# Twelve weight tiles of the convolution stage split on GpSimd, fewer float32 tiles, and a residual without alpha

## The chip, the cores and the metric

The kernel runs on one core of a Trainium2 chip. The metric is the device time of one execution in microseconds (us). The five engines of the core run their own instruction streams and wait for one another by semaphores: TensorE (PE in the profile; its weight loads are PEld), VectorE (DVE), ScalarE (ACT), GpSimd (POOL) and SyncE (SP), which here issues the DMAs.

## The reference, cut to what matters

Two blocks follow one another on x of 256 tokens by 1024 channels, all in float32. The change lies in the second block, in its first half:

```python
h = layer_norm(x) * (1.0 + sc1[:, None]) + sh1[:, None]
proj = h @ w_in                                   # 1024 x 4096
a_val, a_gate, u_pool, gate_a, gate_b = split(proj)   # 512, 512, 512, 1024, 1024 columns ...
ya = a_val * sigmoid(a_gate)
ya = causal_dwconv(ya, w_dw_a, b_dw_a)            # 31 taps, per channel
ya = silu(layer_norm(ya, ln_a_g, ln_a_b))
ya = ya @ w_pw_a
yb = einsum(causal_multiscale_pool(u_pool), w_pool) * pool_scale
merged = sigmoid(gate_a) * ya + sigmoid(gate_b) * yb
mix = merged @ w_out
x = layer_norm(ALPHA * x + g1[:, None] * mix, ln1_g, ln1_b)   # ALPHA = 2 ** 0.25
```

The layer norm adds LN_EPS = 1e-5 to the variance. A common factor on its input drops out of it, if the added number is scaled by the factor's square.

## The kernel before, in words

Activations lie transposed, channels on the 128 partitions and 256 tokens along the free dimension, in blocks of 128 channels. A weight tile is 128x1024 float32 (eight blocks of 128x128, 512 KB), fetched by one DMA from the SP queue into a buffer named `raw`. A product of a 128x128 block with 256 tokens is made in one of two ways:

- **split** (`mm`, lines 237 to 239): weights and activations are each held as a rounded part and a rest (`wh` and `wl` for weights), and three matmuls of the fast float32 form are added: wh by high, wh by low, wl by high. `load` makes the two weight parts from `raw`: ScalarE copies with rounding (line 178, `wh<-raw`), VectorE subtracts (line 179, `wl<-raw,wh`). There are five `wh`, five `wl` and six `raw` buffers.
- **float32** (`mm32`, line 243): one matmul in plain float32 (two records in the trace), with no work for the other engines. Such a tile is fetched straight into a `wh` or `wl` buffer.

The stage of the change runs on PE in this order. `ahead_mm` makes four tiles of w_in in float32 from input that is not yet normed. `k_outer` makes four split tiles. Then come 20 tiles of w_in by `in_tile`: four for the pool branch, all float32, and eight pairs (i = 0 to 7) for the gates; pairs 2, 5 and 6 are split and pairs 0, 1, 3, 4 and 7 are float32, so 14 tiles in all are float32. After pair 3 come 24 matmuls of the pool branch (`pool_out`), which need the pooled sums from VectorE. After pair 7 comes `half_outer("w_pw", ...)`, which needs the normed convolution (`yap`).

Beside it run the 31 taps of the convolution, in two halves of two channel blocks. In 53 of its 62 steps ScalarE multiplies two blocks by their tap (line 1087) and VectorE adds the pair to `acc` (line 1088, 128x512, both inputs in SBUF); in seven VectorE does both (line 1091), and two start the sum (line 1083). The steps are written into the program by a clock that counts planned PE time: `every(0.9, 62, conv)` puts one step every 0.9 us of it. The scheduler of the language then sets the order on each engine. After the last step come the sums of the layer norm on PE (line 1178), its statistics, and `yap` (lines 1186 to 188). For the residual, ScalarE makes `ax` = ALPHA times x (line 1120) in four instructions of 128x512 just ahead of the convolution, and VectorE later adds g1 times mix to it (`fin_mix`).

GpSimd sets a few margins to zero (line 1065, for the pool branch), issues five DMAs, and adds two tiles at the very end (line 1432).

Of the kernel before, what the change touches and what calls it, by code (L numbers as in the profile page):

```python
# [11 lines left out]
F32 = mybir.dt.float32  # L12
F32R = mybir.dt.float32r
I32 = mybir.dt.int32
AF = mybir.ActivationFunctionType
ALU = mybir.AluOpType
ADD, SUB, MUL = ALU.add, ALU.subtract, ALU.mult
AX = mybir.AxisListType

P = 128  # L20
S = 256
D = 1024
DB = D // P
RMS_EPS = 1e-6
LN_EPS = 1e-5
ALPHA = 2.0 ** 0.25
# [55 lines left out]
@with_exitstack  # L82
def tile_kernel(ctx, tc, order, xT, pT, pos, vec, cst, cv, rows, wada, wts, outT):
    nc = tc.nc
    V, A, T = nc.vector, nc.scalar, nc.tensor

    cp = ctx.enter_context(tc.tile_pool(name="cp", bufs=1))
    hp_ = ctx.enter_context(tc.tile_pool(name="half", bufs=14))
# [8 lines left out]
    def nm(s):  # L97
        uid[0] += 1
        return f"{s}_{uid[0]}"
# [4 lines left out]
    def bank2():  # L104
        return bank().rearrange("p (b t) -> p b t", b=2)

    class Blk:

        def __init__(self, nb, dt=F32):
            self.t = [hp_.tile([P, 4, S], dt, tag="half", name=nm("half")) for _ in range((nb + 3) // 4)]  # L110
# [26 lines left out]
    def t1(dt=F32, tag="t1", bufs=8):  # L137
        return tp.tile([P, S], dt, tag=tag, name=nm("t1"), bufs=bufs)
# [3 lines left out]


    class Seq:
        def __init__(self, entries, width=P, parts=True, ready=()):
            self.e, self.w, self.i, self.parts, self.ready = entries, width, 0, parts, list(ready)

        def next(self):
            per = D // self.w
            s = self.i % per  # L150
            if s == 0:
                self.h, self.l = load(self.e[self.i:self.i + per], self.w, self.parts, self.ready.pop(0) if self.ready else None)
            self.i += 1
            sl = slice(s * self.w, (s + 1) * self.w)
            return self.h[:, sl], self.l[:, sl]

    def fetch(entries, width, parts=True, step=D, pinned=False):
        g = len(order)
        order.append((width, list(entries)))
        n = len(entries) * width  # L160
        tag, bufs = (("raw", 6), ("wh", 5), ("wl", 5))[0 if parts else [0, 1][g % len([0, 1])]]
        raw = wp.tile([P, D], F32, tag=tag, name=nm("raw"), bufs=bufs)
        for o in range(0, n, step):
            e = min(n, o + step)
            d = nc.sync.dma_start(out=raw[:, o:e], in_=wts[g, :, o:e])
            if pinned:
                tc.keep_in_program_order(d)
        return raw[:, :n]

    def load(entries, width, parts=True, raw=None):  # L170
        if raw is None:
            raw = fetch(entries, width, parts)
        if not parts:
            return raw, raw
        n = raw.shape[1]
        hi = wp.tile([P, D], F32R, tag="wh", name=nm("wh"), bufs=5)[:, :n]
        lo = wp.tile([P, D], F32R, tag="wl", name=nm("wl"), bufs=5)[:, :n]
        A.copy(hi, raw)  # L178
        V.tensor_sub(lo, raw, hi.bitcast(F32))  # L179
        return hi, lo  # L180

    def nouter(name, ms, kbs, c0=0):
        return [(name, kb * P, c0 + m * P) for m in ms for kb in kbs]
# [19 lines left out]
    def after(us, fn):  # L203
        queue.append((clk[0] + us, fn))
        queue.sort(key=lambda e: e[0])
# [40 lines left out]
    def rhs(pair, kb):  # L246
        return pair[0][kb], pair[1][kb]


    xt = Blk(DB)  # L250
# [27 lines left out]
    V.memset(eps_r, RMS_EPS)  # L278
    eps_l = cp.tile([P, 1], F32, name="eps_l")
    V.memset(eps_l, LN_EPS)  # L280
    A.copy(cp.tile([P, 1], F32, name="first"), eps_l)

    def col(name, i, n=1):
# [81 lines left out]
    def newton(r0, ve, out, eps=None):  # L365
        t = t1()
        V.tensor_mul(t, r0, r0)
        u = t1()
        if eps is None:
            V.tensor_mul(u, ve, t)  # L370
        else:
            V.scalar_tensor_tensor(u, ve, eps, t, ADD, MUL)
        V.scalar_tensor_tensor(out, u, 3.0, r0, SUB, MUL)
        return out
# [6 lines left out]
        A.activation(r0, ps, AF.Abs_reciprocal_sqrt, bias=eps_r, scale=1.0 / n)  # L381
        return newton(r0, ve, t1(tag="nr", bufs=3) if out is None else out)

    def ln_stats(ps, n):

        mu = t1(tag="mu", bufs=2)
        A.activation(mu, ps[0], AF.Copy, scale=1.0 / n)
        msq = t1()
        A.activation(msq, ps[0], AF.Square, scale=1.0 / n)
        var = t1()  # L390
        V.scalar_tensor_tensor(var, ps[1], 1.0 / n, msq, MUL, SUB)
        r0 = t1()
        A.activation(r0, var, AF.Abs_reciprocal_sqrt, bias=eps_l)
        return mu, newton(r0, var, t1(tag="nr", bufs=3), eps=LN_EPS)

    def bc2(t, n=2):
        return t.unsqueeze(1).to_broadcast([P, n, S])
# [2 lines left out]
    mod = cp.tile([P, 48], F32, name="mod")  # L400
# [22 lines left out]
    def every(us, n, step):  # L423

        def run():
            step()
            if n > 1:
                every(us, n - 1, step)
        after(us, run)
# [59 lines left out]
    r0 = {}  # L489
# [251 lines left out]
    xt = post(xt, ys, sums, 0, prep)  # L741
# [56 lines left out]
    seq = Seq([e for kb in range(8) for e in (("mla_kr", kb * P, 0), ("mla_in", kb * P, 768), ("mla_in", kb * P, 896))])  # L798
# [9 lines left out]
    seq = Seq(nouter("mla_in", range(6), range(8)))  # L808
    for i in range(3):
        ps = bank2()  # L810
# [144 lines left out]
    xt = post(xt, ys, sums, 1, prep)  # L955
# [8 lines left out]
    def mod_scales(w):  # L964
        sl = slice(8 * w, 8 * w + 8)
        V.tensor_scalar(s1[:, sl], mod[:, 8 + 24 * w:16 + 24 * w], 1.0, None, ADD)
        V.tensor_scalar(ms[:, sl], s1[:, sl], -0.5, None, MUL)
# [57 lines left out]
    def k_outer(name, tiles, pair):  # L1025
        seq = Seq([(name, kb * P, m * P) for kb in range(8) for m in tiles])
        banks = [bank2() for _ in range(len(tiles) // 2)]
        for kb in range(8):
            for i in range(len(tiles)):
                mm(banks[i // 2][:, i % 2, :], seq.next(), rhs(pair, kb), kb == 0 and i % 2 == 0, kb == 7 and i % 2 == 1)  # L1030
        return banks
# [5 lines left out]
    st = {}  # L1037
# [6 lines left out]
    mu, nrl = st["in"]  # L1044
# [64 lines left out]
    def glu_ahead(i):  # L1109
        gt, gw = ahead_out(pab[2 * i + 1])  # L1110
        A.activation(gt, gt, AF.Sigmoid, bias=gw)
        vt, vw = ahead_out(pab[2 * i])
        V.scalar_tensor_tensor(apad[:, i, 30:], vt, vw, gt, ADD, MUL)
# [1 line left out]
    glu_ahead(0)  # L1115
    modulate(xt, 0, mu, nrl, range(2, 4), hp, hraw)
    glu_ahead(1)
    ax = Blk(DB)
    for i in range(4):
        A.activation(ax.pair(i), xt.pair(i), AF.Copy, scale=ALPHA)  # L1120
    every(0.9, 62, conv)
    pab = k_outer("w_in2", [2, 6, 3, 7], hp)
    for i in (2, 3):
        glu(pab[i - 2], i)

    def in_tile(ps, m, parts):
        seq = Seq(nouter("w_in2", [m], range(8)), parts=parts)  # L1130
        for kb in range(8):
            if parts:
                mm(ps, seq.next(), rhs(hp, kb), kb == 0, kb == 7)
            else:
                mm32(ps, seq.next()[0], hraw[kb], kb == 0, kb == 7)

    for i in range(2):
        ps = bank2()
        for b in range(2):
            in_tile(ps[:, b, :], 8 + 2 * i + b, False)  # L1140
        for b in range(2):
            A.copy(up[2 * i + b][:, 16:], ps[:, b, :])
    pq = Blk(4)
# [61 lines left out]
    for i in range(8):  # L1205
        j = (i + 4) % 8
        ps = bank2()
        for b in range(2):
            in_tile(ps[:, b, :], 12 + 2 * j + b, bool(100 >> i & 1))
        A.activation(sab.pair(j), ps, AF.Sigmoid)  # L1210
        if i == 3:
            pool_out()
# [8 lines left out]

    half_outer("w_pw", yap, fin_pw, 4)

    z = Blk(DB)
    mod_scales(1)
    gs = cp.tile([P, 8], F32, name="gs")
    V.tensor_mul(gs, s1[:, 8:16], col("ln1_g_2", 0, 8))
# [6 lines left out]
    sumz = Sums(True, 1)  # L1234

    def fin_mix(ps, k0, n):
        for b in range(n):
            k = k0 + b
            V.scalar_tensor_tensor(z[k], ps[:, b, :], mod[:, 16 + k:17 + k], ax[k], MUL, ADD)
            A.activation(zs[k][:, :S], z[k], AF.Copy, scale=gs[:, k:k + 1])  # L1240
        if n == 2:
            sumz.feed(z.span(k0, 2))
            if k0 == 4:
                after(4.16, sumz.flush)
        else:
            if k0 == 7:
                drain()
                after(2.03, lambda: (sumz.end(z.span(7, 1), True), ln_1()))
            else:
                after(1.0, lambda: sumz.end(z.span(6, 1), False))  # L1250
# [28 lines left out]
        st["x1"] = ln_stats(sumx.ps[::-1], D)  # L1279

    def ln_1():
        st["z"] = ln_stats(sumz.ps[::-1], D)

        def part(k, n):
            if n == 2:
                sumx.feed(x1.span(k, 2))
        ln_affine(z, st["z"], 0, "ln1_b_2", x1, [1, 3, 5, 7], True, part)
        after(10.0, ln_2)
# [65 lines left out]
    seq = Seq([e for i in range(NA + 2, FB) for e in nouter("w_up", [i, FB + i], range(8))])  # L1354
    for i in range(NA + 2, FB):
        ps = bank2()
# [12 lines left out]
    seq = Seq([("w_down", kb * P, 512 * n) for kb in kbs for n in range(2)], 512)  # L1369

    chunks = [[(0, 512), (512, 512)], [(0, 512), (512, 256), (768, 256)]]
    ps = {(tb, o): bank()[:, :w] for tb in range(2) for o, w in chunks[tb]}
# [27 lines left out]
    for tb in range(2):  # L1400
# [17 lines left out]
        r0 = small(1)  # L1418
# [88 lines left out]
```

## Time and profile before

| what | us |
|---|---|
| median of 3 runs | 845.04 (843.58 to 845.37) |
| the profiled execution | 842.56 |
| its span from first to last instruction | 840.8 |
| PE, PEld busy in the span | 823.7 (98%), 787.2 (94%) |
| DVE, ACT, POOL busy | 702.4 (84%), 552.7 (66%), 9.9 (1%) |

Busy time of an engine is the time in which one of its instructions ran; matmuls overlap, so a busy PE can still differ in pace. The float32 tiles of the stage can be seen in the timeline of PE as unbroken rows of line 243 between 527.9 and 599.7 us. The clock that was granted to TensorE is 1.00 of full speed there, its upper level of 2.4 GHz.

### The profile page before, as it was taken

How to read it: one execution, taken by the hardware profiler on the slowest of the kernel's cores; microseconds unless marked ns; L12 is line 12 of the kernel's file. 1: busy time of each engine (PE TensorE's matmuls, PEld its weight loads, DVE VectorE, ACT ScalarE, POOL GpSimd, SP SyncE). 2: the span in 40 equal slices, each digit the busy share in tenths (PEclk: the TensorE clock that was granted, in tenths of full speed). 3: DMA queues.
4: the chain of work that ended last, by engine and by line, in shares of the span. 5: the costliest groups of instructions: out<-in, count | busy, mean ns of one | idle time of the engine just before them, and what ended most of it. 6: DMA issues, size and time to landing. Idle time of an engine off the chain costs nothing.

```text
span 840.8 us, 15768 instructions
## 1 busy us (share of the span) xinstructions
PE 823.7 (98%) x6114; PEld 787.2 (94%) x6114; DVE 702.4 (84%) x1283; ACT 552.7 (66%) x966; POOL 9.9 (1%) x30
## 2 busy tenths in 40 slices
PE   8999999999999999998999999999999999999995
PEld 6989899999999999998999999899998999999885
DVE  6999798988889978688864767899677888889986
ACT  7655565555676787777754867998755576666551
POOL 0000000000000000000000000000000000000001
PEclk9999999999999999999999999999999999999999
DMA  9876567779556647364354355246363455567822
GB/s 333 330 253 221 206 225 273 253 267 323 174 176 249 250 149 255 135 242 150 109 181 176 118 209 176 76 174 196 132 240 113 148 188 191 179 220 252 274 79 76
DMA packets 46634, 167.48 MB, mean 199 GB/s; under 512 B 5216, under 2 KB 5472, under 8 KB 46560
## 3 DMA queue, kind: packets, MB, share of 16 engines
q1 hardware_dynamic: 45936, 164.38, 55.6%
q0 software_dynamic: 624, 2.10, 0.8%
q8 instruction: 48, 0.79, 0.4%
q14 instruction: 26, 0.21, 0.1%
HBM read 165.41 MB, written 1.05 MB: 198 GB/s over the span
## 4 chain that ended last, share of the span: by engine, by line
PE 51%; DVE 2%; ACT 1%; issue 1%; DVEq 0%
PE ps L238 13%; PE ps L237 13%; PE ps L239 13%; PE ps L243 10%; PE ps L341 1%; PE ps L363 0%; DVE wl L179 0%; PE ps L920 0%; PE ps L1170 0%; DVE t L1434 0%; DVE sm L1415 0%; DVE half L690 0%; DVE t L1411 0%; DVE t L1412 0%; PE ps L1407 0%
## 5 line engine op out<-in xcount | busy, mean ns | idle before, releaser
L237 PE MATMUL ps<-half,wh 128*128 128x256 f32 x1504 | 426.2, 284 | 0.0
L238 PE MATMUL ps<-half,wh 128*128 128x256 f32 x1504 | 424.0, 282 | 0.7 <-DVE half L188 0.6
L239 PE MATMUL ps<-half,wl 128*128 128x256 f32 x1504 | 422.2, 281 | 0.0
L178 ACT CAST wh<-raw 128x1024 fp32r<-128x1024 f32 x233 | 243.5, 1049 | 156.9 <-PE ps L238 99.7
L179 DVE TENSOR_TENSOR wl<-raw,wh 128x1024 fp32r<-128x1024 f32 x233 | 283.1, 1222 | 61.4 <-ACT wh L178 59.3
L238 PEld LDWEIGHTS ps<-half,wh 128*128 128x128 f32 x1504 | 283.6, 189 | 2.0 <-DVE half L188 1.1
L237 PEld LDWEIGHTS ps<-half,wh 128*128 128x128 f32 x1504 | 283.1, 188 | 1.1 <-ACT half L187 0.5
L239 PEld LDWEIGHTS ps<-half,wl 128*128 128x128 f32 x1504 | 284.0, 189 | 0.0
L243 PE MATMUL ps<-half,raw 128*128 128x256 f32 (+2 forms) x384 | 84.9, 380 | 0.0
L243 PEld LDWEIGHTS ps<-half,raw 128*128 128x128 f32 x384 | 72.6, 190 | 9.9
L237 PE MATMUL ps<-wh,half 128*128 128x512 f32 (+1 forms) x202 | 72.7, 361 | 1.0 <-ACT wh L178 1.0
L238 PE MATMUL ps<-wl,half 128*128 128x512 f32 (+1 forms) x202 | 71.1, 352 | 0.5 <-DVE wl L179 0.5
L239 PE MATMUL ps<-wh,half 128*128 128x512 f32 (+1 forms) x202 | 71.1, 352 | 0.0
L413 DVE CUSTOM_DVE_ANT_0 adach<-adach,siluc 128x1024 f32<-128x1024 f32 x48 | 58.6, 1222 | 13.8 <-DMA adach<-in_wada 13.8
L1087 ACT ACTIVATE t<-apad,vec 128x256 f32<-128x256 f32 x106 | 44.3, 500 | 0.5 <-DVE half L1088 0.5
L237 PEld LDWEIGHTS ps<-wh,half 128*128 128x128 f32 x202 | 38.0, 188 | 6.8 <-ACT wh L178 1.8
L238 PEld LDWEIGHTS ps<-wl,half 128*128 128x128 f32 x202 | 38.1, 189 | 6.0 <-DVE wl L179 1.0
L239 PEld LDWEIGHTS ps<-wh,half 128*128 128x128 f32 x202 | 38.0, 188 | 5.6
L1088 DVE TENSOR_TENSOR half<-half,t 128x512 f32<-128x512 f32 x53 | 36.6, 690 | 3.7 <-ACT t L1087 1.8
L187 ACT CAST half<-t 128x256 fp32r<-128x256 f32 (+1 forms) x47 | 20.6, 454 | 18.1 <-DVE t L1347 10.9
L188 DVE TENSOR_TENSOR half<-t,half 128x256 fp32r<-128x256 f32 (+1 forms) x47 | 21.8, 485 | 4.0 <-ACT half L187 3.0
L1342 ACT ACTIVATE t<-ps,vec 128x256 f32<-128x256 f32 x38 | 21.0, 557 | 2.0 <-PE ps L239 1.2
(290 smaller groups left out, 905.5 us busy)
## 6 DMA issues: line engine op xcount, KB each, us to landing
raw<-in_wts SPq DMA_DIRECT2D x257, 512.0 KB, 4.1
adach<-in_wada SPq DMA_DIRECT2D x48, 512.0 KB, 5.0
half<-in_xT SPq DMA_DIRECT2D x4, 256.0 KB, 6.0
half<-in_rows POOLq DMA_DIRECT2D x2, 512.0 KB, 4.5
out<-t SPq DMA_DIRECT2D x4, 256.0 KB, 2.0
cst<-in_cst SPq DMA_DIRECT2D x1, 928.0 KB, 10.6
raw<-in_wts SPq DMA_DIRECT2D x2, 256.0 KB, 4.2
siluc<-in_cv SPq DMA_DIRECT2D x1, 512.0 KB, 8.5
```

Of the source, the lines that this page charges most:

```text
L178: A.copy(hi, raw)
L179: V.tensor_sub(lo, raw, hi.bitcast(F32))
L187: A.copy(hi, src)
L188: V.tensor_sub(lo, src, hi.bitcast(F32))
L237: T.matmul(ps, l[0], r[0], start=first, stop=False)
L238: T.matmul(ps, l[0], r[1], start=False, stop=False)
L239: T.matmul(ps, l[1], r[0], start=False, stop=last)
L243: T.matmul(ps, w, r, start=first, stop=last)
L413: V.tensor_tensor_reduce(ch, ch, sc, 1.0, 0.0, MUL, ADD, mod[:, n:n + 1])
L1087: A.activation(t[:, b, :], apad[:, i0 + b, k:k + S], AF.Copy, scale=w[b])
L1088: V.tensor_add(acc.pair(i0 // 2), acc.pair(i0 // 2), t)
L1342: A.activation(t[:, b, :], ps[:, b, :], AF.Identity, bias=col("b_dw_f_2", m), scale=w[2])
```

## The change

`load` takes a pair of engines. With `by=(G, G)` GpSimd makes both weight parts (lines 181 and 184 of the new kernel), else ScalarE and VectorE do as before (183 and 184). The four pool tiles become split tiles by GpSimd. Of the eight pairs the odd ones (1, 3, 5, 7) are split by GpSimd, pair 6 is split by ScalarE and VectorE, and pairs 0, 2 and 4 are float32. So twelve tiles are split by GpSimd, two by the other engines where six were, and six are float32 where fourteen were. The steps of the convolution are written every 0.85 us of planned PE time. `ax` goes: z becomes x + (g1/ALPHA) times mix, with the number added to the variance divided by ALPHA squared.

```diff
+        first, second = by or (A, V)
+        if first is G:
+            G.tensor_copy(hi, raw)
+        else:
+            A.copy(hi, raw)
+        second.tensor_sub(lo, raw, hi.bitcast(F32))
-        A.copy(hi, raw)
-        V.tensor_sub(lo, raw, hi.bitcast(F32))
...
-    ax = Blk(DB)
-    for i in range(4):
-        A.activation(ax.pair(i), xt.pair(i), AF.Copy, scale=ALPHA)
-    every(0.9, 62, conv)
+    every(0.85, 62, conv)
...
-            in_tile(ps[:, b, :], 8 + 2 * i + b, False)
+            in_tile(ps[:, b, :], 8 + 2 * i + b, True, (G, G))
...
-            in_tile(ps[:, b, :], 12 + 2 * j + b, bool(100 >> i & 1))
+            in_tile(ps[:, b, :], 12 + 2 * j + b, i % 2 or i == 6, (G, G) if i % 2 else None)
...
+    ga = cp.tile([P, 8], F32, name="ga")
+    V.tensor_scalar(ga, mod[:, 16:24], 1.0 / ALPHA, None, MUL)
...
-            V.scalar_tensor_tensor(z[k], ps[:, b, :], mod[:, 16 + k:17 + k], ax[k], MUL, ADD)
+            V.scalar_tensor_tensor(z[k], ps[:, b, :], ga[:, k:k + 1], xt[k], MUL, ADD)
...
-        st["z"] = ln_stats(sumz.ps[::-1], D)
+        st["z"] = ln_stats(sumz.ps[::-1], D, (eps_a, LN_EPS / ALPHA ** 2))
```

Three places show how instructions move. On POOL, before, between the zeroed margin of the convolution's input (`apad`) and the pool branch (`lv` are its sums) there is nothing but a DMA:

```order
L1061 MEMSET apad 128x4x30
L723 DMA t_1041_5824<-in_pT 128x512
L1065 MEMSET lv_6875 128x16
L1065 MEMSET lv_6955 128x16
L1065 MEMSET lv_6958 128x16
L1065 MEMSET lv_6961 128x16
```

On POOL now, the copies and subtractions of the pairs 1 and 3 (the fifth to eighth tile of GpSimd), with the same margins of the pool branch among them:

```order
L181 CAST wh_6940<-raw_6938 128x1024
L184 TENSOR_TENSOR wl_6941<-raw_6938,wh_6940 128x1024
L181 CAST wh_6978<-raw_6976 128x1024
L184 TENSOR_TENSOR wl_6979<-raw_6976,wh_6978 128x1024
L1072 MEMSET lv_6993 128x16
L181 CAST wh_7105<-raw_7103 128x1024
L184 TENSOR_TENSOR wl_7106<-raw_7103,wh_7105 128x1024
L1072 MEMSET lv_7071 128x16
L1072 MEMSET lv_7074 128x16
L181 CAST wh_7143<-raw_7141 128x1024
L1072 MEMSET lv_7077 128x16
L184 TENSOR_TENSOR wl_7144<-raw_7141,wh_7143 128x1024
```

The margins now stand behind splits, and the last split shown stands behind a margin that waits for VectorE.

On ACT at the start of the convolution, before (`sm`, `t` and line 1111 belong to the second input block, `half_6533` and `half_6534` are `ax`):

```order
L1052 ACTIVATE sm_6525<-ps_6375 128x2
L1054 COPY sm_6527<-ps_6375 128x1
L1120 ACTIVATE half_6533<-half_6085 128x512 x2
L1120 ACTIVATE half_6534<-half_6086 128x512
L1111 ACTIVATE t_1163_6521<-t_1163_6521,sm_6519 128x256
L1120 ACTIVATE half_6534<-half_6086 128x512
L1083 ACTIVATE half_6482<-apad,vec 128x256 x2
L1087 ACTIVATE t_1174_6567<-apad,vec 128x256 x2
```

On ACT at the same place now:

```order
L1059 ACTIVATE sm_6527<-ps_6377 128x2
L1061 COPY sm_6529<-ps_6377 128x1
L1090 ACTIVATE half_6484<-apad,vec 128x256
L1094 ACTIVATE t_1172_6563<-apad,vec 128x256
L1094 ACTIVATE t_1176_6582<-apad,vec 128x256
L1094 ACTIVATE t_1177_6595<-apad,vec 128x256
L1118 ACTIVATE t_1163_6523<-t_1163_6523,sm_6521 128x256
L1094 ACTIVATE t_1178_6608<-apad,vec 128x256
```

The four instructions of `ax` are gone, and the first taps stand in their place.

On DVE at the end of the convolution, before (`half_6482` is `acc`; line 1182 is the first step of the norm):

```order
L179 TENSOR_TENSOR wl_7399<-raw_7396,wh_7398 128x1024
L1088 TENSOR_TENSOR half_6482<-half_6482,t_1306_7292 128x512
L1088 TENSOR_TENSOR half_6482<-half_6482,t_1307_7305 128x512
L1088 TENSOR_TENSOR half_6482<-half_6482,t_1308_7318 128x512
L179 TENSOR_TENSOR wl_7429<-raw_7426,wh_7428 128x1024
L1088 TENSOR_TENSOR half_6482<-half_6482,t_1311_7331 128x512
L179 TENSOR_TENSOR wl_7470<-raw_7467,wh_7469 128x1024
L179 TENSOR_TENSOR wl_7506<-raw_7503,wh_7505 128x1024
L1182 TENSOR_TENSOR t_1320_7357<-half_6482,t_1313_7343 128x512
```

On DVE at the same place now:

```order
L184 TENSOR_TENSOR wl_7456<-raw_7453,wh_7455 128x1024
L1095 TENSOR_TENSOR half_6484<-half_6484,t_1299_7285 128x512
L1095 TENSOR_TENSOR half_6484<-half_6484,t_1300_7291 128x512
L1098 SCALAR_TENSOR_TENSOR half_6484<-apad,vec,half_6484 128x256 x2
L1095 TENSOR_TENSOR half_6484<-half_6484,t_1301_7301 128x512
L1095 TENSOR_TENSOR half_6484<-half_6484,t_1306_7322 128x512
L1095 TENSOR_TENSOR half_6484<-half_6484,t_1307_7335 128x512
L1095 TENSOR_TENSOR half_6484<-half_6484,t_1311_7354 128x512
L1095 TENSOR_TENSOR half_6484<-half_6484,t_1312_7367 128x512
L184 TENSOR_TENSOR wl_7555<-raw_7552,wh_7554 128x1024
L1185 TENSOR_TENSOR t_1321_7397<-half_6484,t_1314_7383 128x512
```

The subtractions of weights stand further apart, and the one that came between the last adds stands behind the last. From the first add to the last there were nine of them on DVE, and there are three.

## Rows read from the trace of the kernel before

**Rows 1.** The page: span, and busy time of each engine.
```profile
span 840.8 us, 15768 instructions
PE 823.7 (98%) x6114; PEld 787.2 (94%) x6114; DVE 702.4 (84%) x1283; ACT 552.7 (66%) x966; POOL 9.9 (1%) x30
```

**Rows 2.** Windows of the convolution stage; us, busy us (and instructions) per engine, clock, DMA.
```profile
510.00:527.00 17.00, 17.00 (x121) 16.15 (x120) 11.33 (x26) 14.83 (x37) 0.00 (x0) 1.00 0.54 187
527.00:590.00 63.00, 63.00 (x371) 57.90 (x370) 60.83 (x116) 59.18 (x135) 0.90 (x8) 1.00 0.43 148
590.00:600.00 10.00, 9.95 (x51) 8.58 (x51) 6.78 (x11) 7.58 (x13) 0.00 (x0) 1.00 0.65 211
```

**Rows 3.** Timeline of PE: start us, us, line, what, count [idle before].
```profile
527.92 27.79 PE L243 MATMUL ps<-half,raw 128*128 128x256 f32 x128
...
555.35 0.47 PE L237 MATMUL ps<-half,wh 128*128 128x256 f32 x1
...
562.94 7.07 PE L243 MATMUL ps<-half,raw 128*128 128x256 f32 x32
569.65 0.47 PE L237 MATMUL ps<-half,wh 128*128 128x256 f32 x1
...
579.39 0.47 PE L237 MATMUL ps<-half,wh 128*128 128x256 f32 x1
...
590.90 1.89 PE L243 MATMUL ps<-half,raw 128*128 128x256 f32 x8
592.62 1.03 PE L1178 MATMUL ps<-half,ones 128*128 128x256 f32 x4
...
599.74 0.74 PE L237 MATMUL ps<-half,wh 128*128 128x256 f32 x4
```

**Rows 4.** Groups by line and form on DVE, 527 to 590 us; busy us, mean ns | idle.
```profile
L1088 DVE TENSOR_TENSOR half<-half,t 128x512 f32<-128x512 f32 x53 | 36.6, 690 | 3.7 <-ACT t L1087 1.8
L179 DVE TENSOR_TENSOR wl<-raw,wh 128x1024 fp32r<-128x1024 f32 x10 | 12.2, 1221 | 0.0
L1203 DVE SCALAR_TENSOR_TENSOR half<-ps,vec,half 128x256 f32<-128x256 f32 x8 | 3.2, 478 | 0.0
```

**Rows 5.** Timeline of DVE and ACT at the start and end of the convolution.
```profile
522.70 1.68 ACT L1120 ACTIVATE half<-half 128x512 f32<-128x512 f32 x3
524.69 0.62 ACT L1120 ACTIVATE half<-half 128x512 f32<-128x512 f32 x1
527.12 1.49 DVE L1088 TENSOR_TENSOR half<-half,t 128x512 f32<-128x512 f32 x2 [1.82 <-ACT t L1087]
...
588.13 1.22 DVE L179 TENSOR_TENSOR wl<-raw,wh 128x1024 fp32r<-128x1024 f32 x1
589.26 0.68 DVE L1088 TENSOR_TENSOR half<-half,t 128x512 f32<-128x512 f32 x1
589.98 0.63 ACT L1175 ACTIVATE t<-half 128x512 f32<-128x512 f32 x1 [0.72 <-DVE half L1088]
...
599.72 0.43 DVE L188 TENSOR_TENSOR half<-t,half 128x256 fp32r<-128x256 f32 x1 [0.85 <-ACT half L187]
```

**Rows 6.** Groups by line and form on POOL, the whole span.
```profile
L1432 POOL TENSOR_TENSOR t<-t,half 128x512 f32<-128x512 f32 x2 | 3.0, 1492 | 12.7 <-DVE t L1431 12.7
L767 POOL MEMSET kr<- 64x256 f32 x4 | 1.2, 306 | 148.7 <-DVE t L560 148.5
L1065 POOL MEMSET lv<- 128x16 f32 x10 | 1.1, 112 | 134.1 <-DVE sm L1154 122.1 <-DVE lv L1150 12.0
```

**Rows 7.** Line 1432: duration ns least/median/most; first and last start.
```profile
L1432 POOL TENSOR_TENSOR t<-t,half x2: 1252/1492/1732, 831.8 to 833.5; 128x512 f32<-128x512 f32 x2
```

**Rows 8.** Timeline beside line 1432.
```profile
831.69 0.69 DVE L1431 TENSOR_TENSOR t<-t,half 128x512 f32<-128x512 f32 x1
831.77 2.95 POOL L1432 TENSOR_TENSOR t<-t,half 128x512 f32<-128x512 f32 x2 [12.68 <-DVE t L1431]
832.30 0.42 DVE L1412 SCALAR_TENSOR_TENSOR t<-ps,t 128x256 f32<-128x256 f32 x1
```

More of the change, by code (lines that the diff above doesn't have):

```diff
@@ L84, in tile_kernel @@
     nc = tc.nc
-    V, A, T = nc.vector, nc.scalar, nc.tensor
+    V, A, T, G = nc.vector, nc.scalar, nc.tensor, nc.gpsimd
     cp = ctx.enter_context(tc.tile_pool(name="cp", bufs=1))
@@ L144, in tile_kernel, with __init__ @@
     class Seq:
-        def __init__(self, entries, width=P, parts=True, ready=()):
-            self.e, self.w, self.i, self.parts, self.ready = entries, width, 0, parts, list(ready)
+        def __init__(self, entries, width=P, parts=True, ready=(), by=None):
+            self.e, self.w, self.i, self.parts, self.ready, self.by = entries, width, 0, parts, list(ready), by
         def next(self):
@@ L151, in next @@
             if s == 0:
-                self.h, self.l = load(self.e[self.i:self.i + per], self.w, self.parts, self.ready.pop(0) if self.ready else None)
+                self.h, self.l = load(self.e[self.i:self.i + per], self.w, self.parts, self.ready.pop(0) if self.ready else None, self.by)
             self.i += 1
@@ L168, in fetch, with load @@
         return raw[:, :n]
-    def load(entries, width, parts=True, raw=None):
+    def load(entries, width, parts=True, raw=None, by=None):
         if raw is None:
@@ L280, in tile_kernel @@
     V.memset(eps_l, LN_EPS)
+    eps_a = cp.tile([P, 1], F32, name="eps_a")
+    V.memset(eps_a, LN_EPS / ALPHA ** 2)
     A.copy(cp.tile([P, 1], F32, name="first"), eps_l)
@@ L382, in rms_neg2, with ln_stats @@
         return newton(r0, ve, t1(tag="nr", bufs=3) if out is None else out)
-    def ln_stats(ps, n):
+    def ln_stats(ps, n, eps=(eps_l, LN_EPS)):
         mu = t1(tag="mu", bufs=2)
@@ L392, in ln_stats @@
         r0 = t1()
-        A.activation(r0, var, AF.Abs_reciprocal_sqrt, bias=eps_l)
-        return mu, newton(r0, var, t1(tag="nr", bufs=3), eps=LN_EPS)
+        A.activation(r0, var, AF.Abs_reciprocal_sqrt, bias=eps[0])
+        return mu, newton(r0, var, t1(tag="nr", bufs=3), eps=eps[1])
     def bc2(t, n=2):
@@ L1124, in tile_kernel, with in_tile @@
         glu(pab[i - 2], i)
-    def in_tile(ps, m, parts):
-        seq = Seq(nouter("w_in2", [m], range(8)), parts=parts)
+    def in_tile(ps, m, parts, by=None):
+        seq = Seq(nouter("w_in2", [m], range(8)), parts=parts, by=by)
         for kb in range(8):
```

## The prediction

> **What bounds the kernel now.** I read the page's engine line first: PE is busy for 823.7 of 840.8 us [rows 1], so time is saved only where PE's own work shrinks, and is lost wherever something makes PE wait. Then I cut the stage into windows [rows 2]. From 527 to 590 us PE is busy for all 63.0 us at granted clock 1.00 (the 2.4 GHz level), and beside it DVE is busy for 60.83 and ACT for 59.18. So two more engines are nearly full in this stage, and POOL is empty (0.90). Last I followed the convolution to its end. Its last add starts on DVE at 589.26, ACT squares the result at 589.98 [rows 5], PE takes it for the sums at 592.62, and the first matmul of w_pw, which needs the normed result, starts at 599.74 [rows 3], in the same moment as the rest of its first block on DVE (599.72) [rows 5]. So PE and the chain of the convolution arrive together: both must get shorter for a gain, and either alone can lose.
>
> **PE's own work.** Eight tiles turn from float32 into split. The first eight float32 tiles run from 527.92 to 555.35, 3.43 us each; the pair from 562.94 to 569.65 gives 3.36 each; the four split tiles from 579.39 to 590.90 take 2.88 each [rows 3]. Four tiles at 0.55 and four at 0.48 are 4.1 us less. The changes from float32 to split, where the first matmul takes longer (0.47 for 0.28), stay three in number, so they cancel.
>
> **ScalarE.** The four `ax` instructions ahead of the convolution go. They were on its path: the first add waited 1.82 us for ACT [rows 5]. I take 1.8 us. The later z has the same shape with x in place of `ax`; `ga` and the second epsilon are two tiny instructions far from the stage's end, and cost nothing beside DVE work that PE does not wait for.
>
> **VectorE's own work.** Of the ten weight subtractions between 527 and 590 [rows 4] one starts after the last add, at 589.86; nine stand before it. In the new order three do: four went to GpSimd and two of w_pw now stand behind the last add. One takes 1.13 us of DVE's queue (from 588.13 to 589.26) [rows 5], so six are 6.8 us less. ACT loses as many casts, so it does not become the bound.
>
> **GpSimd's work.** No row shows a 128x1024 copy or subtraction on POOL. For the subtraction the nearest row is the 128x512 add, 1.252 us at its shorter [rows 7]; twice that, less one fixed part of about 0.1 (the 16-column MEMSET takes 0.112 [rows 6]), is 2.4. For the rounding copy the lower end is the rate of a MEMSET (0.306 at 256 columns, 0.112 at 16, so 0.81 ns a column: 0.93 at 1024) and the upper end twice the add, 2.5. I take 1.0, since a copy with one input is nearer to the MEMSET than to an add with two. A tile costs 3.4 us, at most 4.9; twelve cost 41. GpSimd itself is in time: an odd pair comes once per two float32 and two split tiles, 12.6 us, and needs 6.8 (at most 9.8). For the first four PE asks for the last some 8.6 us after 527.9; five `wh` buffers let GpSimd begin while `k_outer` still runs. The margins of the pool branch, now behind splits on POOL (line 1065), can come up to a tile late, and DVE's pool adds queue behind them; I count this inside the next term.
>
> **What GpSimd does to VectorE.** This term decides. Of the two adds on line 1432 the first took 1.732 us and the second 1.252 [rows 7]. The first was started at 831.77, 0.08 after a VectorE instruction with two SBUF inputs (L1431, 831.69 to 832.38) [rows 8]. If it stood still until that one had read its inputs, at about 832.25, the 0.48 us are explained to within 0.05. The VectorE instruction kept its 0.69, and the next one on VectorE, with one input from PSUM, ran beside POOL in its usual 0.42 [rows 8]. I read it as: a GpSimd instruction and a VectorE instruction with two SBUF inputs do not run at the same time. The other reading is a cost of the first use on POOL, which would say nothing about the stage.
>
> The Trainium skill, page "SBUF — State Buffer", section "Who interferes with whom", says the same: VectorE with two SBUF inputs contends with a GpSimd instruction that reads SBUF, and whichever is first holds the shared ports for its whole instruction. This trace agrees for GpSimd waiting (0.48 us); no run so far shows VectorE waiting. By this rule the sum below stands; without it the first rival holds.
>
> In the stage nearly all VectorE work is of this kind: 53 adds of `acc` alone are 36.6 us, against 3.2 us of line 1203, which reads PSUM [rows 4]. So GpSimd's time is put in line with VectorE's. Before 527 DVE has 5.7 us free (17.0 less 11.33) [rows 2], room for two of the twelve tiles. Ten remain, 34 us. From these go the 3.2 us of line 1203 and the 2.2 us in which DVE was idle from 527 to 590.
>
> **The sum.** The convolution's end moves by -1.8 - 6.8 + 34 - 3.2 - 2.2 = +20.0 us. PE has then run out of tiles, so the square no longer waits behind tiles on PE (ready at 590.6, taken at 592.62): -2. PE starts w_pw 18 us later, and its own 4.1 vanish in that wait. The profiled execution took 842.56 with 840.8 of span and 1.8 around it; it becomes 860.6. It lay 2.5 under the median of the runs, 845.04, so I predict 863. With the copy at 2.5 ten tiles add 15: 878. With four tiles before 527, and margins for DVE time that is not reading, it is 854.
>
> The Trainium skill, page "GPSIMD Engine Reference", section "3.1 Elementwise — side-by-side cycle accounting", has 4497 ns for a subtraction's kind at 2048 columns; half of it, 2.25, is an estimate that would make the ten tiles 1.5 us shorter. No run so far shows the size.
>
> **Rivals.**
> *GpSimd works beside VectorE for nothing.* Then PE's 4.1 us come out in full, since the convolution has 1.8 + 6.8 = 8.6 us to give and needs 4.1: 841.0 (839 to 843). For it: POOL is empty, DVE is relieved by more than PE. Against it: the 0.48 us would be the cost of a first use that fits the overlap by chance. This is the gain, chance 0.28.
>
> *Half a price.* The engines share instead of excluding one another, and VectorE loses half as much, 14 us. It is free up to 8.6 - 4.1 = 4.5 us and a loss from some 9 us on: at 14 it is about 5 us slower, 850; between 7 and 10.5 us it is no change. For it: one row is thin evidence that the wait is whole. Against: a sharing GpSimd would have lost 0.3 of the 0.6 us of overlap, not 0.48. Chance 0.12, a third of it no change and a sixth a gain.
>
> *Only GpSimd waits.* VectorE is never held up and GpSimd creeps through its gaps. Then the convolution ends on time, but `wl` is late and PE waits for line 184 instead. The same two loads share the same time, so the price is the same 18 us at another place. I hold it inside the forecast, whose chance is 0.60 in all (0.45 with VectorE blocked).
>
> **How the numbers follow.** What a measurement of this kernel can tell from no change is about 0.2%, 1.7 us. Faster: 0.28 and 0.02 of the half price, 0.30. Same: 0.04. Slower: 0.60 and 0.06, 0.66. The forecast's own range is 854 to 878. Since the gain has 0.28, the range for 8 in 10 reaches from 839.5 to 879, which leaves out some 0.05 at either end.
>
> **What would show it.** In the changed profile: the pool tiles and pairs 1, 3, 5 and 7 at 2.88 us a tile where their weights are there (PE's term); POOL rows on line 181 of about 1.0 us alone and on line 184 of about 2.4, longer where they waited; VectorE adds on line 1095 whose longest are over 1.5 us where all were about 0.69; PE idle by some 20 us in one or two places, at pair 3 or `pool_out` (waiting for the pooled sums) and ahead of w_pw. The forecast is wrong if the adds on line 1095 keep 0.69 us while POOL runs, or if PE has no idle time before w_pw; then the time is near 841.

## The result, and the profile after

The changed kernel takes 873.76 us (median of four, 870.42 to 876.48) where the kernel before took 844.31 beside it on the same chip (843.35 to 845.37): ratio 1.0350, 95% interval 1.0325 to 1.0375. That is 29.5 us slower. The forecast was 863, 18 us slower.

The page of the changed kernel, span and engines (beside [rows 1]); the profiled execution took 876.48:

```profile
span 874.7 us, 15934 instructions
PE 826.1 (94%) x6178; PEld 790.3 (90%) x6178; DVE 729.7 (83%) x1281; ACT 547.4 (63%) x958; POOL 60.8 (7%) x54
```

PE is no longer full: its busy time fell from 98% to 94% of the span. Where it stood is told by its waits, 500 to 660 us (columns: what waited, for whom; total us, times, longest):

```profile
PE ps L1173 <- DVE half L1095: 17.9, 1, 17.9
PE ps L1181 <- DVE half L1095: 9.7, 1, 9.7
PE ps L243 <- DVE half L193: 0.5, 1, 0.5
```

Two stops make 27.6 us, and both wait for an add of the convolution. Lines 1173 and 1181 are the sums of its layer norm over the first and the second half. The windows of the stretch show the same (columns as in [rows 2]):

```profile
560.00:570.00 10.00, 0.75 (x4) 0.33 (x2) 10.00 (x19) 6.60 (x16) 7.32 (x6) 0.78 0.15 53
570.00:580.00 10.00, 1.38 (x3) 1.17 (x4) 10.00 (x20) 5.56 (x13) 1.60 (x5) 0.50 0.43 158
610.00:620.00 10.00, 1.11 (x3) 0.94 (x4) 9.52 (x11) 2.59 (x5) 2.81 (x1) 0.67 0.41 157
```

PE is busy for 0.75, 1.38 and 1.11 us of ten while DVE never rests. Before, PE was full here [rows 2]. Beside the idle time look at the clock: 0.50 and 0.67, where it was 1.00. What DVE did in that time is told by groups of line and form (busy us, mean ns; beside [rows 4]); first DVE 515 to 635 us, then POOL:

```profile
L1095 DVE TENSOR_TENSOR half<-half,t 128x512 f32<-128x512 f32 x53 | 49.5, 937 | 3.5 <-ACT t L1094 1.1
L1206 DVE SCALAR_TENSOR_TENSOR half<-ps,vec,half 128x256 f32<-128x256 f32 x8 | 3.2, 476 | 0.0
...
L184 POOL TENSOR_TENSOR wl<-raw,wh 128x1024 fp32r<-128x1024 f32 x12 | 34.4, 2867 | 0.9
L181 POOL CAST wh<-raw 128x1024 fp32r<-128x1024 f32 x12 | 16.9, 1405 | 113.8 <-PE ps L248 109.2 <-PE ps L243 4.7
```

The same 53 adds took 36.6 us before; now their mean is 937 ns for 690, while line 1206, which reads PSUM, kept its 476. One line's durations (least/median/most) say that the adds are not slower in general, but that some of them stood still (nine took 1.34 to 2.86 us):

```profile
L1095 DVE TENSOR_TENSOR half<-half,t x53: 673/692/2864, 539.9 to 618.1; 128x512 f32<-128x512 f32 x53
```

The adds hold 12.9 us of what VectorE lost. Other VectorE instructions with two SBUF inputs were held too: the taps on line 1098 took 11.1 us where they took 6.7, and the modulation ahead of the convolution was stretched as well.

The timeline shows who stood for whom. POOL, and DVE beside it, 565 to 571 us:

```profile
565.72 5.50 POOL L184 TENSOR_TENSOR wl<-raw,wh 128x1024 fp32r<-128x1024 f32 x1
...
567.39 0.68 DVE L1095 TENSOR_TENSOR half<-half,t 128x512 f32<-128x512 f32 x1
568.00 0.40 DVE L1155 SCALAR_TENSOR_TENSOR half<-lv,upad 128x240 f32<-128x240 f32 x1
568.32 0.68 DVE L1095 TENSOR_TENSOR half<-half,t 128x512 f32<-128x512 f32 x1
568.92 2.34 DVE L1157 TENSOR_TENSOR sm<-lv,cst 128x16 f32<-128x16 f32 x1
```

While DVE ran one instruction with two SBUF inputs after another, POOL's subtraction stood (5.50 us where its shortest is 2.40). At about 568.8 POOL got its turn (its end, 571.22, less 2.40), and the VectorE instruction of 16 columns that came next, 0.16 us elsewhere, took 2.34. Each side stands still until the other's instruction is done.

### The profile page after: what moved, and what is told of

It is laid out like the page before. It is cut to its first block, busy times and chain, and to the rows that moved or that the text cites. A ratio compares the mean times of both kernels' runs of the same rounds, so it can differ in the third digit from the quotient of the medians.

```text
span 874.7 us, 15934 instructions
## 1 busy us (share of the span) xinstructions
PE 826.1 (94%) x6178; PEld 790.3 (90%) x6178; DVE 729.7 (83%) x1281; ACT 547.4 (63%) x958; POOL 60.8 (7%) x54
## 4 chain that ended last, share of the span: by engine, by line
PE 41%; DVE 11%; issue 2%; ACT 1%; DVEq 0%; ACTq 0%
PE ps L243 12%; PE ps L242 12%; PE ps L244 12%; DVE half L1095 4%; PE ps L248 4%; PE ps L348 1%; DVE half L1098 1%; DVE wl L184 1%; DVE half L1005 1%; PE ps L1181 0%; PE ps L1173 0%; DVE t L994 0%; DVE t L1064 0%; DVE half L1206 0%; PE ps L927 0%
## 5 line engine op out<-in xcount | busy, mean ns | idle before, releaser
L242 PE MATMUL ps<-half,wh 128*128 128x256 f32 x1568 | 444.7, 284 | 0.0
L244 PE MATMUL ps<-half,wl 128*128 128x256 f32 x1568 | 440.7, 281 | 2.8 <-DVE wl L184 2.8
L243 PE MATMUL ps<-half,wh 128*128 128x256 f32 x1568 | 442.3, 282 | 1.1 <-DVE half L193 1.0
L183 ACT CAST wh<-raw 128x1024 fp32r<-128x1024 f32 x229 | 238.7, 1049 | 152.9 <-PE ps L243 97.9
L184 DVE TENSOR_TENSOR wl<-raw,wh 128x1024 fp32r<-128x1024 f32 x229 | 278.4, 1223 | 60.9 <-ACT wh L183 58.8
L244 PEld LDWEIGHTS ps<-half,wl 128*128 128x128 f32 x1568 | 295.9, 189 | 3.3 <-DVE wl L184 3.2
L243 PEld LDWEIGHTS ps<-half,wh 128*128 128x128 f32 x1568 | 295.6, 189 | 2.7 <-DVE half L193 1.6
L242 PEld LDWEIGHTS ps<-half,wh 128*128 128x128 f32 x1568 | 295.6, 189 | 0.7
L248 PE MATMUL ps<-half,raw 128*128 128x260 f32 (+2 forms) x256 | 57.4, 382 | 0.0
L248 PEld LDWEIGHTS ps<-half,raw 128*128 128x128 f32 x256 | 48.6, 191 | 6.9
L1095 DVE TENSOR_TENSOR half<-half,t 128x512 f32<-128x512 f32 x53 | 49.5, 937 | 3.5 <-ACT t L1094 1.1
L184 POOL TENSOR_TENSOR wl<-raw,wh 128x1024 fp32r<-128x1024 f32 x12 | 34.4, 2867 | 0.9
```

Source lines behind the costliest of these rows:

```text
L184: second.tensor_sub(lo, raw, hi.bitcast(F32))
L242: T.matmul(ps, l[0], r[0], start=first, stop=False)
L243: T.matmul(ps, l[0], r[1], start=False, stop=False)
L244: T.matmul(ps, l[1], r[0], start=False, stop=last)
L248: T.matmul(ps, w, r, start=first, stop=last)
L1095: V.tensor_add(acc.pair(i0 // 2), acc.pair(i0 // 2), t)
```

## The experiments

All were timed against the kernel before, beside it on the same chip (medians 843.7 to 844.2).

**The residual without alpha, alone.** The kernel before with that part of the change and nothing else.

```diff
-    ax = Blk(DB)
-    for i in range(4):
-        A.activation(ax.pair(i), xt.pair(i), AF.Copy, scale=ALPHA)
...
```

> The kernel before with only alpha taken out of the residual (no ax on ScalarE, steps still every 0.9). Exclusion theory (a GpSimd instruction that reads SBUF and a VectorE instruction with two SBUF inputs do not run together): PE stays full, so the 1.8 us that the convolution gains are not needed, 844 (843 to 845). Rival (the new residual itself costs, by its later z or by x being kept longer): 846 or more.

845.29 us, ratio 1.0012 (0.9992 to 1.0032): no difference that can be told, and PE has no wait in the stage. The loss is not in this part.

**The splits, made by ScalarE and VectorE.** The changed kernel without GpSimd.

```diff
-            in_tile(ps[:, b, :], 8 + 2 * i + b, True, (G, G))
+            in_tile(ps[:, b, :], 8 + 2 * i + b, True)
...
-            in_tile(ps[:, b, :], 12 + 2 * j + b, i % 2 or i == 6, (G, G) if i % 2 else None)
+            in_tile(ps[:, b, :], 12 + 2 * j + b, i % 2 or i == 6)
```

> The changed kernel with the twelve tiles split by ScalarE and VectorE in place of GpSimd. Exclusion theory: VectorE takes 12 x 1.13 = 13.6 us in place of GpSimd's 34 and more, nothing else is in its way; the convolution ends about 3 us later than before and PE has 4 us less to do: 847 (843 to 853). Rival (the loss lies in the float32 tiles given up, in weights that come late or in the order of the buffers, whoever splits): near the changed kernel, 865 to 876.

855.32 us, 1.0118 (1.0094 to 1.0142): 11 us slower than before, 8 above the expected 847 and outside its range, but 18 better than the change. The longest add of line 1095 is 696 ns: none stands still. PE's waits say what the 11 us are:

```profile
PE ps L242 <- ACT wh L183: 5.3, 1, 5.3
PE ps L242 <- ACT half L192: 3.8, 1, 3.8
PE ps L244 <- DVE wl L184: 1.6, 1, 1.6
```

Two engines that are nearly full can't take twelve more tiles either; but GpSimd's help costs more than that.

**GpSimd at work for nobody.** The kernel before without alpha, and GpSimd beside it on the first twelve float32 tiles, writing into scratch that nothing else reads; the steps stay at 0.9 us. Three kinds of work of about the same length: copy and subtract; write only; copy only.

```diff
+                    nc.gpsimd.tensor_copy(own, seq.h)
+                    nc.gpsimd.tensor_sub(own2, seq.h, own.bitcast(F32))
```
```diff
+                    nc.gpsimd.tensor_copy(own[:, :1], seq.h[:, :1])
+                    for _ in range(4):
+                        nc.gpsimd.memset(own.bitcast(F32), 0.0)
```
```diff
+                    for _ in range(3):
+                        nc.gpsimd.tensor_copy(own, seq.h)
```

> No alpha, and GpSimd copies and subtracts the first twelve float32 tiles of the stage into two scratch tiles that nobody reads; PE, ScalarE and VectorE do what they do in x1. Exclusion theory: ten tiles of 3.6 us are put in line with VectorE: 1.8 gained, 36 lost, some 5 hidden: +25 to +33 over x1, 869 to 877, with VectorE adds of over 2 us. Rival (first use, or waits in queues on GpSimd's results): nothing waits for these, so 844 to 846 and every add 0.69.

> As x3, but for each of the twelve tiles GpSimd reads one column of it and then sets the scratch tile to zero four times (128x1024 each, about as long as a copy and a subtraction). Exclusion theory in the form that only reading counts: VectorE is not held up, 844 to 848 (the pool branch's margins queue behind up to four such instructions). Rival (any busy GpSimd slows VectorE, or the margins behind long instructions are the cause): as slow as x3.

> The kernel before without alpha in the residual, in which GpSimd copies each of the first twelve float32 tiles three times into a buffer that nothing reads, and subtracts nothing: 36 copies of 128x1024, one SBUF input each, 37 to 45 us of GpSimd as with copies and subtractions (875). Exclusion by every GpSimd instruction that reads SBUF: 862 to 875, with adds of the convolution stretched to nearly 2 us. Rival (only a GpSimd instruction with two SBUF inputs excludes): 844 to 847, adds at 0.69.

| GpSimd's work | GpSimd busy | time | ratio (interval) |
|---|---|---|---|
| copies and subtractions | 45 us | 874.53 | 1.0348 (1.0316 to 1.0380) |
| writes | 53 us | 845.08 | 1.0013 (0.9996 to 1.0029) |
| copies | 46 us | 867.04 | 1.0252 (1.0217 to 1.0287) |

All three as exclusion expected. For each, GpSimd's main group and the adds of the convolution, in the order of the table:

```profile
L1139 POOL TENSOR_TENSOR own<-raw,own 128x1024 fp32r<-128x1024 f32 x12 | 30.3, 2528 | 0.9
...
L1090 DVE TENSOR_TENSOR half<-half,t x53: 675/691/2832, 541.7 to 622.1; 128x512 f32<-128x512 f32 x53
```
```profile
L1140 POOL MEMSET own<- 128x1024 f32 x48 | 45.7, 953 | 2.5
...
L1090 DVE TENSOR_TENSOR half<-half,t x53: 674/691/933, 530.6 to 594.2; 128x512 f32<-128x512 f32 x53
```
```profile
L1139 POOL CAST own<-raw 128x1024 fp32r<-128x1024 f32 x36 | 45.9, 1275 | 94.7 <-PE ps L243 93.0
...
L1090 DVE TENSOR_TENSOR half<-half,t x53: 673/692/1522, 534.5 to 615.6; 128x512 f32<-128x512 f32 x53
```

The first loses as much as the change though nobody waits for GpSimd, no tile of PE is changed and the steps keep their spacing. So the loss is not weights that GpSimd makes too late. It reaches PE by another way than in the change, though. Most of PE's waits there are for the weights that ScalarE and VectorE split, and ScalarE's own waits are mostly for VectorE:

```profile
PE ps L237 <- ACT wh L178: 8.8, 1, 8.8
PE ps L239 <- DVE wl L179: 8.0, 3, 5.1
```

What the run shares with the change is VectorE's loss, and not the place where PE stands for it. The second run shows that the cause is not GpSimd's being busy: as much time spent on writing cost nothing that can be told. The third shows that one SBUF input of GpSimd is enough; the longest add then is 0.83 us over the usual, less than one copy, where with subtractions it is 2.14 over.

**The running sum in PSUM.** The other way round: GpSimd works as in the change, and VectorE's adds have one SBUF input. Done to the changed kernel, to the kernel before (the control), and to the changed kernel with GpSimd on the odd pairs alone.

```diff
+            ap = bank2()
...
-                    V.tensor_add(acc.pair(i0 // 2), acc.pair(i0 // 2), t)
+                    V.tensor_add(acc.pair(i0 // 2) if k == 30 else ap, ap, t)
```

> The changed kernel, with the convolution's running sum in PSUM instead of SBUF: the 53 adds and the taps of VectorE then have one SBUF input, as line 1206 has, which kept its 0.48 us beside GpSimd; only the last step of each half writes the SBUF block. GpSimd's twelve tiles stay. Exclusion theory: the adds keep their usual time (about 0.69 us, none over 1 us) beside GpSimd, and most of the 29 us goes; what is left is the modulation ahead of the convolution and the few subtractions of weights and sums of the pool branch, which still read SBUF twice: 848, between 840 and 858. Rival 1 (GpSimd slows whatever VectorE does, or takes SBUF's ports from every reader): 866 to 876, and adds of 2 to 3 us remain. Rival 2 (PE waits for the weights that GpSimd makes, about 3.7 us a tile, whatever the adds do): above 858, with PE's waits at POOL's line 184.

> The kernel before with the convolution's running sum in PSUM and nothing else: the control for the run of the changed kernel with that edit. Both theories: 844 (842 to 847), since the convolution ends where PE is still full. Should an add from PSUM take over 0.85 us instead of 0.69, 53 of them would lose more than the convolution's slack and this goes above 847.

> The changed kernel with the running sum in PSUM, and the four pool tiles in float32 as before: GpSimd splits only the eight tiles of pairs 1, 3, 5 and 7, so that nothing of it runs beside the modulation ahead of the convolution. Exclusion theory: hardly any VectorE instruction with two SBUF inputs is left beside GpSimd, and PE's own work is 2 us shorter than before: 843, between 840 and 848. If GpSimd slows VectorE whatever its inputs are: eight twelfths of the loss, 860 to 866.

Changed kernel 856.61, ratio 1.0136 (1.0109 to 1.0162): above the expected 848, in its range. Control 849.76, 1.0059 (1.0042 to 1.0075): above its range, missed. Odd pairs alone 848.57, 1.0051 (1.0032 to 1.0069): just above its range. The adds of the first, beside GpSimd's twelve tiles:

```profile
L1096 DVE TENSOR_TENSOR ps<-ps,t x51: 681/699/700, 533.9 to 597.8; 128x512 f32<-128x512 f32 x51
L1096 DVE TENSOR_TENSOR half<-ps,t x2: 676/677/678, 566.2 to 599.7; 128x512 f32<-128x512 f32 x2
```

Not one stands still, and the change's price over the control is 7 us (856.6 less 849.8), where it was 29. Against the kernel before it is still 13. In the control an add takes 0.70 us and not 0.69; what it loses is the last add 4.5 us later (two more subtractions of weights came to stand ahead of it, which is about half of that) and then 3.5 us of PE in front of w_pw. With the four early tiles gone too, the price over the control is nothing (848.6). So the 7 us come with the early tiles, which run beside the modulation ahead of the convolution, and that still reads SBUF twice: counted as in the account below, the first add comes 6.2 us later than before with these tiles and 0.5 sooner without them.

**Part of the tiles.** The sum back in SBUF; GpSimd on the eight tiles of the odd pairs alone, or on the four pool tiles alone.

```diff
-            in_tile(ps[:, b, :], 8 + 2 * i + b, True, (G, G))
+            in_tile(ps[:, b, :], 8 + 2 * i + b, False)
...
```
```diff
-            in_tile(ps[:, b, :], 12 + 2 * j + b, i % 2 or i == 6, (G, G) if i % 2 else None)
+            in_tile(ps[:, b, :], 12 + 2 * j + b, i == 6)
```

> The changed kernel with the four pool tiles in float32 as before: GpSimd splits only the eight tiles of pairs 1, 3, 5 and 7. Exclusion with the measured price of 3.7 us a tile: 8 x 3.7 = 29.6 us in line, less 6.8 (fewer weight subtractions), 1.8 (alpha), 3.2 and 2.2 as in the prediction: the convolution ends 15.6 us later, so 859 (854 to 864), with no stretched instruction in the modulation. Rival (the loss lies mainly in the early tiles, which delay the start of the convolution): 845 to 850.

> The changed kernel with the odd pairs in float32: GpSimd splits only the four pool tiles, early; pair 6 alone is split by ScalarE and VectorE. If early tiles hide in VectorE's free time before the convolution, as the prediction took it for two of them: 843 to 846. If they cost in full because they hold the modulation that the convolution waits for: 4 x 3.7 = 14.8 us, less 1.8 for alpha and about 8 for seven subtractions that VectorE no longer has, of which some stand late: 5 us later, 849 (846 to 854).

Odd pairs 869.04, ratio 1.0305 (1.0284 to 1.0326); pool tiles 857.22, 1.0171 (1.0140 to 1.0202). Both came out slower than any of the theories. Yet the convolution did about what was expected: against the lateness that each execution already had at 492 us (0.9 and 1.0), its last add ended 15.9 us later with the odd pairs (expected 15.6) and 2.6 with the pool tiles (expected about 5). The missing time is on PE. Its waits, odd pairs, then pool tiles:

```profile
PE ps L1173 <- DVE half L1095: 11.2, 1, 11.2
PE ps L1181 <- DVE half L1095: 9.2, 1, 9.2
PE ps L243 <- DVE half L193: 1.6, 1, 1.6
```
```profile
PE ps L1173 <- DVE half L1095: 8.0, 1, 8.0
PE ps L1181 <- DVE half L1095: 0.9, 1, 0.9
```

With the pool tiles alone the convolution ends nearly on time, and PE still loses 8.0 us at the sums of its first half. It has the tiles to do, but they stand behind the sums in its queue; and since it has no slack later, what it lost stays lost.

**The place of the stop.** Two numbers: the second sums 8.4 us of planned PE time later in the changed kernel; and both sums later (4.0 and 3.4) in the version with the sum in PSUM and the odd pairs.

```diff
-                    after(0.6, ln_a)
+                    after(9.0, ln_a)
```
```diff
-                    after(0.6, ln_a)
+                    after(4.0, ln_a)
...
-        after(2.0, sums)
+        after(6.0, sums)
```

> The changed kernel with one number altered: the second sums of the convolution's layer norm are written 9 instead of 0.6 us of planned PE time after the last step, so that PE does all of pair 7 but seven blocks before it comes to them. In the changed kernel PE stood 9.7 us at these sums with two tiles of pair 7 behind them, had a low granted clock for 4 us after it, and came to w_pw 13 us after the last add instead of 9.8. Theory (part of the loss is the place of the stop, not GpSimd's time): the stop of 9.7 us is mostly gone and w_pw comes 3 to 5 us sooner: 870 (867 to 872). Rival (the stop only moves, since w_pw waits for the norm anyway): 873 to 876, with a new wait of PE ahead of w_pw of some 9 us.

> The version in which the running sum is in PSUM and GpSimd splits only the odd pairs (848.6), with the two places where PE stood for the sums (3.6 and 0.6 us) written 4 and 3.4 us of planned PE time later. Theory: the stops go, and the convolution ends about where it ended before: 844 (841 to 847), PE's own 2 us shorter work showing at best in part. Rival (the convolution's chain sets w_pw whatever PE does meanwhile): 848 to 850.

The first gave 873.26, ratio 1.0350 (1.0324 to 1.0375): nothing, as the rival had it. The stop of 9.7 us fell to 1.0, and a new one stands ahead of w_pw, where PE waits for the norm:

```profile
PE ps L1173 <- DVE half L1095: 15.1, 1, 15.1
PE ps L242 <- ACT half L192: 7.8, 1, 7.8
```

The expectation had misread the changed kernel: it came to w_pw 15.3 us after the last add and not 13, and behind its stop stood nearly all of pairs 6 and 7, not two tiles. Here w_pw came 12.3 us after the last add (617.42 to 629.74), 3.0 sooner; but in this execution the last add itself came 1.8 us later in the stage, so what the new place is worth by itself is not shown.

The second gave 842.82, ratio 0.9985 (0.9970 to 1.0000): some 5.8 us less than the same kernel with its stops (848.57, ratio 1.0051), 31 better than the change, and by its interval the equal of the kernel before or a little better. PE's whole wait for the sums is

```profile
PE ps L1174 <- DVE half L1096: 1.0, 1, 1.0
```

and its granted clock is 1.00 in every window of ten us from 540 to 640. So a late place for the sums helped where the convolution was nearly on time, and brought nothing that can be told where it was 22 us late.

## Why the prediction was right, and where its size was off

The direction and the mechanism were right: GpSimd's reading was put in line with VectorE's, the convolution ended late, and PE stood. The size was not: 29.5 us where 18 were forecast. That 873.8 still lies between 854 and 878 is in part luck. The upper end was set by a copy of 2.5 us, and the copy took 1.04; the room was filled by something else, for the most part by the way from the last add to w_pw, which the sum had wrong.

**The account of the loss.** For each run I took the lateness of the last matmul against the kernel before, less the lateness already there at 492 us (6.6 us in the changed kernel, 0.6 to 7.8 in the others: executions scatter there, also where that part is not changed). To that stand PE's waits from 500 to 660 us, and PE's own work saved by split tiles (0.55 us for each pool tile, 0.48 for each of the others, net of those that went back to float32 [rows 3]):

| kernel | stage lost | PE waits | work saved | rest |
|---|---|---|---|---|
| changed | 27.4 | 28.1 | 4.1 | 3.4 |
| second sums later | 28.8 | 27.5 | 4.1 | 5.4 |
| odd pairs only | 23.6 | 22.0 | 1.9 | 3.5 |
| pool tiles only | 12.0 | 8.9 | 0.3 | 3.4 |
| sum in PSUM | 13.5 | 12.9 | 4.1 | 4.7 |
| copies only, for nobody | 22.0 | 15.9 | 0 | 6.1 |
| PSUM, odd pairs | 3.1 | 4.2 | 1.9 | 0.8 |
| the same, sums later | -1.1 | 1.4 | 1.9 | -0.6 |

Lost is what PE waits, less what it saves, plus a rest (lost less waits plus saved), which is there where PE stood long. PE's timeline in the changed kernel shows the rest, at the sums after each stop (beside the 1.03 us of the same form in [rows 3]):

```profile
578.62 2.04 PE L1173 MATMUL ps<-half,ones 128*128 128x256 f32 x4 [17.87 <-DVE half L1095]
...
618.89 2.07 PE L1181 MATMUL ps<-half,ones 128*128 128x256 f32 x4 [9.70 <-DVE half L1095]
...
621.83 1.88 PE L1181 MATMUL ps<-t,ones 128*128 128x256 f32 x4
```

PE came back at granted clock 0.50, the 1.2 GHz level, until about 582.3 and 623.2: 3.7 and 4.3 us at half speed are 4.0 us of lost work, beside a rest of 3.4.

**Term by term.**

- *PE's own work, -4.1.* The rows bear it out: split blocks run at 0.12 us from matmul to matmul, as before. As predicted it vanished in the waits; it came out only where PE had none (last line of the table).
- *Alpha, -1.8.* Sized too large. In the five runs that have no `ax`, and where GpSimd reads no whole tile ahead of the convolution, the first add came 0.5 us sooner, counted from the lateness at 492 us. Of the 1.82 us that it had waited for ACT [rows 5] it still waits 1.21, for the first taps. In the run without alpha alone:

```profile
534.45 3.08 DVE L1090 TENSOR_TENSOR half<-half,t 128x512 f32<-128x512 f32 x4 [1.21 <-ACT t L1089]
```

- *The weight subtractions, -6.8.* Six did leave the stretch, as counted; their price was not seen apart, and two of w_pw did not leave for free (below).
- *GpSimd's work, 3.4 us a tile.* Undisturbed it is 1.04 and 2.40, so 3.44. This was sized right.
- *Exclusion, 34 us.* The deciding step, and right: [rows 7] and [rows 8] carried it on one row. The Trainium skill, page "SBUF — State Buffer", section "Who interferes with whom", has the contention of VectorE's two-input instructions for GpSimd instructions that read SBUF and not for those that only write, and none for a VectorE instruction with at most one SBUF input outside the modes that use two ports. The runs agree on all three (867.0, 845.1 and adds of 0.70 us), and show what the prediction's trace did not, VectorE waiting (2.34 us for 0.16). Its size: the last add came 28.9 us later, 22.3 of it in the stage, for 20.0 predicted. Put back what was taken off (alpha's 0.5 as measured, 6.8, 3.2, 2.2) and 35.0 of GpSimd's 41.3 us went into line, for 34; the last three were not measured apart.
- *Two tiles hidden before 527.* About right: with the pool tiles alone the first add came 6.2 us later, 6.7 with alpha's 0.5 put back, so 7.1 of their 13.8 us were hidden. The rest delays the start of the convolution; the stretched instructions there are those of the modulation.
- *From the last add to w_pw, -2.* This is the step that failed: "PE has then run out of tiles, so the square no longer waits". It went from 9.8 to 15.3 us (618.84 to 634.16), +5.5 where I had -2; of the 9.4 us that the stage lost beyond 18, 7.5 lie here and 2.3 in the convolution's end (and 0.4 came back after it). PE had not run out: the sums stand in its queue right behind pair 5, so it stood 9.7 us with nearly all of pairs 6 and 7 still to do (95 of 96 matmuls, some 11 us at 0.12), at first at half speed. The square, ready at 619.5, was taken at 621.83, so it still waited. PE then went from pair 7 into w_pw without a wait. The first block of the norm was ready little sooner, at 632 to 633 us: the two subtractions of w_pw that I counted as moved away stand, with their casts on ACT, between its steps. So two chains, PE's tiles and the norm, ended within 2 us of each other, and shortening one alone could not bring much. DVE and ACT after the last add (beside [rows 5]):

```profile
625.74 0.42 DVE L380 SCALAR_TENSOR_TENSOR t<-t,t 128x256 f32<-128x256 f32 x1
626.89 1.22 DVE L184 TENSOR_TENSOR wl<-raw,wh 128x1024 fp32r<-128x1024 f32 x1 [0.72 <-ACT wh L183]
628.03 1.28 DVE L1186 TENSOR_TENSOR t<-t,t 128x512 f32<-128x512 f32 x2
...
632.42 0.76 DVE L193 TENSOR_TENSOR half<-t,half 128x256 fp32r<-128x256 f32 x2 [1.48 <-ACT half L192]
...
628.63 1.05 ACT L183 CAST wh<-raw 128x1024 fp32r<-128x1024 f32 x1 [1.78 <-PE ps L243]
629.71 1.28 ACT L1189 ACT_TABLE_LOAD   x1
632.00 0.70 ACT L192 CAST half<-t 128x256 fp32r<-128x256 f32 x2
```

Before, line 1183 followed line 373 within 0.5 us (597.12 and 597.58); here a subtraction is between them, and a cast ahead of the table load.

- *Where PE stands.* "At pair 3 or `pool_out` and ahead of w_pw", some 20 us: it was 27.6, the larger part in pair 2, at the first sums. I had not looked where in PE's order the first half of the convolution is asked for. With it I would have seen a second, earlier stop, and that the gain in PE's work can't be kept in front of it.
- *The clock.* Not in the sum at all; 3 to 4 us by the working above.

**The rivals.** "GpSimd works beside VectorE for nothing" falls with 874.5 for work that nobody needs. "Half a price" falls with the rows: an instruction either keeps its length (673 ns is the shortest add beside GpSimd, and 0.69 us was all of them before) or waits until the other's is done. "Only GpSimd waits" falls with VectorE's 2.34 us; both wait, whoever came second.

What stays open: the profiled executions account for 27.4 us in the stage and the medians for 29.5; the difference is within the interval (27.4 to 31.7 us) and the scatter of the first 200 us, and I could not assign it.

## What to carry to other kernels

Count the time of GpSimd instructions that read SBUF as VectorE's own, wherever VectorE is full of instructions with two SBUF inputs; if GpSimd must work there, keep one of VectorE's operands in PSUM (here 29 us over the kernel before fell to 13, and 7 over a control that was itself 6 us slower) or keep GpSimd away from the stretch. On an engine that is full and works in order, look up what each instruction that can be late has behind it: the stop costs its whole length, and the low clock after it some us more. Moving such a point later was worth it when the late chain was nearly on time (some 5.8 us here), and brought nothing when the chain was 22 us behind.

## What the runs showed of the hardware that I had not expected

- A GpSimd copy with a single SBUF input excludes VectorE as a subtraction does (46 us of copies: 23 us slower). It takes 1.04 us for 128x1024 by itself and up to 2.12 in the change, where it met such VectorE work; the subtraction 2.40, and up to 5.50.
- GpSimd's writes left VectorE's adds alone: 48 MEMSETs of 128x1024, 0.95 us each, in the same stretch, left the time at 1.0013. But one SBUF input is no safeguard for every VectorE instruction: a TENSOR_SCALAR of 128x8, 0.17 us before, took 1.03 us beside a MEMSET and 1.01 beside a GpSimd copy (rows below: writes only, copies only). Why this form was held where the adds were not, no run here shows.
- A VectorE add of 128x512 takes 0.70 us with one input and the output in PSUM and 0.69 all in SBUF, so the adds cost no more there. The kernel before with its sum in PSUM was still 6 us slower (849.76), with its last add 4.5 us later.
- The lower clock after a stop: 1.03 us of sums became 2.04 to 2.07, for 4.3 and 3.7 us after stops of 9.7 and 17.9 us. It also followed a stop of 3.5 us in the control with the sum in PSUM, where PE came back at 605.09: the granted clock was 0.50 from 605 to 609 and 0.74 from 609 to 613.

```profile
567.57 1.03 DVE L1239 TENSOR_SCALAR sm<-gs 128x8 f32<-128x8 f32 x1
...
589.02 1.01 DVE L1240 TENSOR_SCALAR sm<-s 128x8 f32<-128x8 f32 x1
```
